# One hybrid decoder step on one core: VectorE's work in the recurrence in program order, some operations handed out later

## The chip, the cores and the metric

One core of a Trainium2 chip runs the whole program. The metric is the device time of one execution in microseconds; three executions of the kernel before gave 1235.94, 1236.01 and 1239.28 us (median 1236.01).

## The reference, cut to what matters

576 tokens (512 of a prompt, 64 of eight sample sequences) go through one layer with three branches, all from one input projection. Everything is fp32.

```
xn = RMSNorm(x);  proj = xn @ w_in                      # 105 column blocks of 128
y_conv = B * conv3(C * h) * silu(g_conv)
y_rwkv = RWKV7(token-shifted r, k, v, decay, icl) * silu(g_rwkv)
y_mem  = softmax(q K^T / sqrt(d)) V * silu(g_mem)       # 4 heads, 256 memory tokens
merged = sum_i sigmoid(m_i) * (y_i @ w_branch[i])
y = RMSNorm_final(x + merged @ w_out)

# RWKV7, for each of 16 heads, one token after another:
sa = S @ kk
S  = S * w  - outer(sa, kk * a) + outer(v, k)
o  = S @ r
```

## The kernel before, in words

**Products.** A product (`mm`, line 233) takes 128 columns of a weight against the 576 tokens. Each fp32 operand is split into a high and a low part, so a product is 48 matmuls of 128 x 288: eight blocks of the contraction, three terms, two halves of the tokens. `mm` yields after each pair of matmuls. One such yield is called a **step** here: a product is 24 steps, two matmuls each.

**Lanes.** `drive` (line 278) runs a main generator; after each of its steps it gives each of five lanes one turn, in the order chain, post, merge, invert, prep. A lane that yields n sits out n turns, so `yield n` puts n + 1 steps between what is before it and after it. So the matmuls of the recurrence come between the matmuls of the products, at places that count in steps, not in time.

**The order on each engine.** Around everything stands `tc.manual_schedule(engines=MANUAL)` with TensorE alone (line 31): TensorE takes its instructions in the order in which the program hands them out. The order on VectorE, ScalarE, GpSimd and the DMA queues is the framework's planner's, which places instructions when it thinks that their inputs are there. Each engine's queue then runs in the order so fixed, each instruction waiting for its own inputs.

**The recurrence** is done in chunks of 64 tokens, nine to a pair of heads (eight of the prompt, one for all samples), for eight pairs of heads p = 0 to 7. `rwkv_main` (line 950) gives it its main stream: first `lora`, then for each p the projections of r, k (after `want[0] >= p`) and v, and between them a filler: eight convolution blocks of four products, eight queries, then tanh gates for the later branches (`early_gates`, list `EARLY`, line 403) for as long as any lane is busy. A gate made early is stored to DRAM and fetched by `branch` (line 1014); one that was not made early is computed there. For a pair p:

- `shift` (line 421) mixes a projected tile with its predecessor token: ScalarE writes `E`, VectorE copies two edges out of PSUM (lines 431, 432) and combines tile and `E` (lines 437 to 445). `proj` marks the tile in `got`.
- `prep` (line 565) makes decays, keys and masks: exponentials on ScalarE, a scan, then `while moved[0] < p - 1 or done[0] < p - 1` (chain p - 2 must be over), four wide operations (lines 613 to 617: `fkb`, `fva`, `eF`, `fkb`), 9 steps later the matmuls of line 633, masks `msk`, and DMAs through DRAM (`scr`) into `nin`. Then it sets `want` and queues `invert`.
- `invert` (line 686): yields 28, then solves 32 x 32 triangles in 31 dependent rounds, `tmp = Z * nin` and `Z = Z - tmp` (lines 696, 698), both on VectorE, one round per step (`yield 0`). DMAs through `sco` put the result into `msk`. It queues `merge` with a due step 92 steps on (`READY`).
- `merge` (line 711): after the due step two VectorE transposes of `msk` (line 786), matmuls (lines 796, 803), and so on; 25 steps after the due step `chain` is queued.
- `chain` (line 833): nine chunks of 16 steps. In each, line 869 multiplies by the state `sb`, VectorE adds the result into `vu` (line 871), 8 steps later lines 882 and 887 use `vu`, VectorE updates `sb` in two operations (line 893), and 8 steps later line 869 of the next chunk uses `sb`. So every 8 steps TensorE needs what VectorE was given 8 steps before. One chain runs at a time.
- `post` (line 907): sample states and the group norm.

After the recurrence come attention beside branch 0, then gates and branches 2 and 1 as plain products, then the output product with `wout`'s weights and the final norm.

Of the kernel before, what the change touches and what calls it, by code (L numbers as in the profile page):

```python
# [61 lines left out]
def pr(t):  # L62
    return v3(t)[:, :, 0:256]
# [22 lines left out]
def hybrid_step(ctx, tc, x_nat, x_t, mem_t, w_in, w_br, w_mk, w_mv, w_o, kc, vc, swkv,  # L86
# [188 lines left out]
    chain_lane, post_lane, prep_lane, inv_lane, mrg_lane = (Lane() for _ in range(5))  # L275
    lanes = [chain_lane, post_lane, mrg_lane, inv_lane, prep_lane]

    def drive(main):
        for _ in main:
            TICK[0] += 1  # L280
            for ln in lanes:
                ln.step()

# [116 lines left out]
    def etile(tag, dt=F32, **k):  # L400
        return el.tile([128, T], dt, name="e" + tag, tag=tag, **k)

    EARLY = [(i, j) for i in (1, 2) for j in range(8)]
    gates = {}
    QT = ("r", "k", "A", "B", "C", "D", "E1", "F")
    qt = []
# [9 lines left out]
    with ExitStack() as rctx:  # L416
# [4 lines left out]
        def shift(ps, idx, out, flat=True):  # L421
            E = shf.tile([128, 513 + 72], F32, name="E", tag="E")
            Es = E[:, 513:585].rearrange("p (b t) -> p b t", t=9)
            mu = pc("mu", idx)
            G.memset(E[:, 0:1], 0.0)
            act(E[:, 1:513].rearrange("p (h t) -> p h t", h=2), ps[:, :, 0:256], scale=mu)
            act(Es[:, :, 0:1], shp[:, idx, :].unsqueeze(2), scale=mu)
            for hf in range(2):
                act(Es[:, 4 * hf:4 * hf + 4, 1:9],
                    ps[:, hf, 256:288].rearrange("p (b t) -> p b t", t=8), scale=mu)  # L430
            V.tensor_copy(sho[:, idx, 0:1], ps[:, 1, 255:256])
            V.tensor_copy(sho[:, idx, 1:9].rearrange("p (h b) -> p h b", h=2),
                          ps[:, :, 256:288].rearrange("p h (b t) -> p h b t", t=8)[:, :, :, 7])
            om = omm[:, idx:idx + 1]
            if flat:
                out = c9(out)
                stt(out[:, 0:8].rearrange("p (h c) t -> p h (c t)", h=2), ps[:, :, 0:256], om,
                    E[:, 0:512].rearrange("p (h t) -> p h t", h=2), ALU.mult, ALU.add)
            for hf in range(2):
                if not flat:  # L440
                    stt(out[:, 4 * hf:4 * hf + 4], c9(ps[:, hf, 0:256]), om,
                        c9(E[:, 256 * hf:256 * hf + 256]), ALU.mult, ALU.add)
                stt(out[:, 8, 32 * hf:32 + 32 * hf].rearrange("p (b t) -> p b t", t=8),
                    ps[:, hf, 256:288].rearrange("p (b t) -> p b t", t=8), om,
                    Es[:, 4 * hf:4 * hf + 4, 0:8], ALU.mult, ALU.add)

        def conv(j):
            U = cvp.tile([128, 514 + 80], F32, name="U")
            Us = U[:, 514:594].rearrange("p (b t) -> p b t", t=10)
            G.memset(U[:, 0:2], 0.0)  # L450
            G.tensor_copy(Us[:, :, 0:2], scv[:, j])
            ps = yield from mm(w_in[WC + j])
            c = cvp.tile([128, T], F32, name="c")
            act(v3(c), m3(ps))
            yield "tile"
            ps = yield from mm(w_in[WH + j])
            tt(V, U[:, 2:514].rearrange("p (h t) -> p h t", h=2), ps[:, :, 0:256], pr(c), ALU.mult)
            for hf in range(2):
                tt(V, Us[:, 4 * hf:4 * hf + 4, 2:10],
                   ps[:, hf, 256:288].rearrange("p (b t) -> p b t", t=8),  # L460
                   v3(c)[:, hf, 256:288].rearrange("p (b t) -> p b t", t=8), ALU.mult)
            G.tensor_copy(cvo[:, j, 0:2], U[:, 512:514])
            G.tensor_copy(cvo[:, j, 2:18].rearrange("p (b t) -> p b t", t=2), Us[:, :, 8:10])
            if j == 6:
                yc.extend(slots("s3b", 2))
            y = yc[j]
            w = [pc("cw%d" % i, j) for i in range(3)]

            def up(i):
                return U[:, i:i + 512].rearrange("p (h t) -> p h t", h=2)  # L470

            def us(i, hf):
                return Us[:, 4 * hf:4 * hf + 4, i:i + 8]

            def ys(hf):
                return v3(y)[:, hf, 256:288].rearrange("p (b t) -> p b t", t=8)

            cb = pc("conv_b", j)
            act(pr(y), up(0), AF.Identity, scale=w[0], bias=cb)
            for hf in range(2):  # L480
                act(ys(hf), us(0, hf), AF.Identity, scale=w[0], bias=cb)
            for i in (1, 2):
                stt(pr(y), up(i), w[i], pr(y), ALU.mult, ALU.add)
                for hf in range(2):
                    stt(ys(hf), us(i, hf), w[i], ys(hf), ALU.mult, ALU.add)
            yield "tile"
            ps = yield from mm(w_in[WB + j])
            stt(v3(y), m3(ps), 0.5, v3(y), ALU.mult, ALU.mult)
            yield "tile"
            ps = yield from mm(w_in[WG + j])  # L490
            th = cvp.tile([128, T], F32, name="c")
            act(v3(th), m3(ps), AF.Tanh, scale=0.5)
            stt(v3(th), v3(th), 1.0, m3(ps), ALU.add, ALU.mult)
            tt(G, y, y, th, ALU.mult)
            yield "tile"


# [17 lines left out]
        def lora():  # L515
            act(blkr, cc("blk"))
            ps = yield from mm(w_in[WP + 24])

            lor, swp = etile("A"), etile("B")
            shift(ps, 24, lor)  # L520
            act(lor[up], lor[up], AF.Tanh)
            S.dma_start(out=swp[dn], in_=lor[up])
            S.dma_start(out=swp[up], in_=lor[dn])
            stacks(lx, lor, swp)
            for o, (a, b) in enumerate(((lor, swp), (swp, lor))):
                tt(V, xlo[o][up], a[up], lx[o][up].bitcast(F32), ALU.subtract)
                tt(V, xlo[o][dn], b[dn], lx[o][dn].bitcast(F32), ALU.subtract)
# [24 lines left out]

        def proj(p, i):
            ps = yield from mm(w_in[WP + 8 * i + p])
            if i < 2:
                t = etile("rk"[i])
                shift(ps, 8 * i + p, t)
            else:
                t = fvas[p]
                shift(ps, 8 * i + p, t[:, :, 0, :], flat=False)  # L560
            got[p, i] = t

        got, fvas = {}, {}

        def prep(p):
            r, k = got[p, 0], got[p, 1]
            fs = slice(p * 128, p * 128 + 128)
            A = etile("A")
# [20 lines left out]
            act(D, D, AF.Exp, scale=CD / 2)  # L589
            act(F, k, scale=pc("k_k", p))  # L590
            act(E1, B, AF.Identity, scale=kah[:, p:p + 1], bias=kah[:, 8 + p:9 + p])
            yield 3
            tt(V, E1, E1, k, ALU.mult)
            act(A, A, AF.Exp, scale=-CD / 2)

# [88 lines left out]
            yield 0  # L684

        def invert(p, msk, mu_, nin, sco, fkb, fva, pcl, rn):
            yield 28

            zp = pch.tile([128, 512], F32, name="c")
            Z = zp[0:108, 0:352].rearrange("p (m k) -> p m k", k=32)  # L690
            tmp = rw.tile([108, 11 * 32], F32, name="tmp", bufs=1)
            act(zp[0:108, 0:352], zini)
            for j in range(31):
                nm, nk = j // 3 + 1, 31 - j
                tv = tmp[:, 0:nm * nk].rearrange("p (m k) -> p m k", k=nk)
                tt(V, tv, Z[:, 0:nm, j:j + 1].to_broadcast([108, nm, nk]),
                   nin[:, j:j + 1, j + 1:32].to_broadcast([108, nm, nk]), ALU.mult)
                tt(V, Z[:, 0:nm, j + 1:32], Z[:, 0:nm, j + 1:32], tv, ALU.subtract)
                yield 0
            sq3 = sco.rearrange("u (m q) k -> q u m k", q=3)  # L700
            act(tmp, zp[0:108, 0:352])
            zo = tmp.rearrange("p (m k) -> p m k", k=32)
            for q in range(3):
                S.dma_start(out=sq3[q], in_=zo[36 * q:36 * q + 36])
            for bl in range(2):
                q0 = 64 + 32 * bl
                S.dma_start(out=mu_[q0:q0 + 32, :, 32 * bl:32 * bl + 32],
                              in_=sco[18 * bl:18 * bl + 18, 0:32, :].rearrange("u s t -> s u t"))
            mrg_lane.q.append(merge(p, msk, fkb, fva, pcl, rn, TICK[0] + READY))
# [197 lines left out]
        def post(p, S0, vu8, chk8, pcl):  # L907
# [19 lines left out]
            V.tensor_reduce(st[:, 0, :], of, axis=AX.X, op=ALU.add)  # L927
            V.tensor_scalar(st[:, 0, :], st[:, 0, :], 1.0 / 64, None, op0=ALU.mult)
            tt(G, of, of, st[:, 0, :].unsqueeze(2).to_broadcast([128, 10, 64]), ALU.subtract)
            yield 1  # L930
            sq = rw.tile([128, 10, 64], F32, name="sq", tag="mb", bufs=1)
            act(sq, of, AF.Square)
            V.tensor_reduce(st[:, 1, :], sq, axis=AX.X, op=ALU.add)
            G.tensor_scalar(st[:, 1, :], st[:, 1, :], 1.0 / 64, 64e-5, op0=ALU.mult, op1=ALU.add)
            tt(G, st[:, 2, :], st[:, 1, :], nhalf[:, 0:10], ALU.pow)
# [58 lines left out]
                else:  # L994
                    return

        drive(rwkv_main())

    S.dma_start(out=o_conv, in_=cvo)
    S.dma_start(out=o_shift, in_=sho)  # L1000
# [256 lines left out]
            yield lag  # L1257


    prep_lane.q.append(wout(0, 27))  # L1260
    drive(branch(1, *parts, merged=(mgh, mgl)))
    for _ in wout(1, 0):
        pass
# [139 lines left out]
```

## Time and profile before

| | before |
|---|---|
| median of three executions | 1236.01 us |
| profiled execution, its own time | 1235.45 us |
| its span, first to last instruction | 1233.6 us |
| TensorE busy | 1186.9 us, 96% of the span |
| VectorE, ScalarE, GpSimd busy | 587.0, 524.9, 573.8 us |
| mean granted TensorE clock | 0.994 |

The profiled execution's own time is 1.85 us over its span (what lies ahead of the first and behind the last instruction). Matmuls overlap in TensorE's pipeline and their ends are modelled, so idle time of TensorE is a wait, while a busy TensorE is not one at its peak. Lines 93, 96 and 99 are helpers (`tt`, `stt`, `act`) that issue most of the work of VectorE, GpSimd and ScalarE; there the tiles' names tell which operation it is. In them `e` stands ahead of tiles of `etile`, and `c`, `tmp`, `nin` are the inversion's `Z`, `tmp`, `nin`.

### The profile page before, as it was taken

How to read it: one execution, taken by the hardware profiler on the slowest of the kernel's cores; microseconds unless marked ns; L12 is line 12 of the kernel's file. 1: busy time of each engine (PE TensorE's matmuls, PEld its weight loads, DVE VectorE, ACT ScalarE, POOL GpSimd, SP SyncE). 2: the span in 40 equal slices, each digit the busy share in tenths (PEclk: the TensorE clock that was granted, in tenths of full speed). 3: DMA queues.
4: the chain of work that ended last, by engine and by line, in shares of the span. 5: the costliest groups of instructions: out<-in, count | busy, mean ns of one | idle time of the engine just before them, and what ended most of it. 6: DMA issues, size and time to landing. Idle time of an engine off the chain costs nothing. (4 is left out here: it accounts for less than half of the span.)

```text
span 1233.6 us, 25594 instructions
## 1 busy us (share of the span) xinstructions
PE 1186.9 (96%) x10158; PEld 1100.8 (89%) x10158; DVE 587.0 (48%) x1514; ACT 524.9 (43%) x1120; POOL 573.8 (47%) x521
## 2 busy tenths in 40 slices
PE   7999979999899999999989999999999999999997
PEld 7798979989798988988879898889899999999976
DVE  7856866468675686647673315213113100134233
ACT  6563446435463544546344435333233222233222
POOL 4535532555535465454543545333334454446642
PEclk9999989999999999999999999999999999999999
DMA  8642222132321322222322225653632222225522
GB/s 290 213 126 72 70 72 63 59 91 58 91 65 53 89 68 84 90 86 70 110 80 74 69 71 171 195 181 123 208 97 87 80 84 86 78 86 161 161 105 78
DMA packets 93056, 129.39 MB, mean 105 GB/s; under 512 B 36988, under 2 KB 41320, under 8 KB 92936
## 3 DMA queue, kind: packets, MB, share of 16 engines
q1 hardware_dynamic: 55888, 110.20, 28.3%
q10 hardware_dynamic: 37048, 17.56, 5.4%
q8 instruction: 80, 1.31, 0.5%
q14 instruction: 40, 0.33, 0.1%
HBM read 115.96 MB, written 11.47 MB: 103 GB/s over the span
## 5 line engine op out<-in xcount | busy, mean ns | idle before, releaser
L93 POOL TENSOR_TENSOR wl<-w,wh 128x512 fp32r<-128x512 f32 x274 | 366.5, 1340 | 490.0 <-ACT wh L99 451.4
L245 PE MATMUL m<-xh,wh 128*128 128x288 f32 x1680 | 370.4, 302 | 0.5 <-ACT vst L99 0.5
L245 PE MATMUL m<-xl,wh 128*128 128x288 f32 x1680 | 369.4, 301 | 0.0
L245 PE MATMUL m<-xh,wl 128*128 128x288 f32 x1680 | 365.2, 299 | 0.0
L99 ACT ACTIVATE wh<-w 128x512 fp32r<-128x512 f32 x290 | 180.5, 627 | 294.2 <-PE m L245 169.1
L245 PEld LDWEIGHTS m<-xh,wh 128*128 128x128 f32 x1680 | 268.8, 189 | 8.6 <-issue 3.7
L245 PEld LDWEIGHTS m<-xl,wh 128*128 128x128 f32 x1680 | 269.2, 189 | 6.4 <-issue 2.9
L245 PEld LDWEIGHTS m<-xh,wl 128*128 128x128 f32 x1680 | 269.4, 189 | 3.0 <-issue 2.1
L96 DVE SCALAR_TENSOR_TENSOR ev<-ev,m 128x576 f32<-128x576 f32 x32 | 24.2, 755 | 168.4 <-PE m L245 110.3
L245 PE MATMUL m<-yh,wh 128*128 128x288 f32 x384 | 82.9, 297 | 0.0
L245 PE MATMUL m<-yh,wl 128*128 128x288 f32 x384 | 82.8, 297 | 0.0
L245 PE MATMUL m<-yl,wh 128*128 128x288 f32 x384 | 82.8, 297 | 0.0
L245 PEld LDWEIGHTS m<-yh,wl 128*128 128x128 f32 x384 | 61.7, 188 | 2.1 <-issue 2.1
L245 PEld LDWEIGHTS m<-yl,wh 128*128 128x128 f32 x384 | 61.7, 188 | 2.1 <-issue 2.1
L245 PEld LDWEIGHTS m<-yh,wh 128*128 128x128 f32 x384 | 61.7, 189 | 2.1 <-issue 2.1
L93 DVE TENSOR_TENSOR c<-c,tmp 108x84 f32<-108x84 f32 (+23 forms) x248 | 56.6, 228 | 5.4
L93 DVE TENSOR_TENSOR tmp<-c,nin 108x84 f32<-108x84 f32 (+23 forms) x248 | 54.8, 221 | 6.7 <-issue 1.2
L96 DVE SCALAR_TENSOR_TENSOR sb<-o,pcl,sb 64x64 f32<-64x64 f32 x112 | 31.6, 282 | 52.1 <-PE o L887 46.0
L99 ACT ACTIVATE osb<-o 64x128 f32<-64x128 f32 x72 | 19.7, 274 | 52.3 <-DVE sb L96 30.5
L93 DVE TENSOR_TENSOR vu<-o,vu 64x128 f32<-64x128 f32 x56 | 15.9, 284 | 46.6 <-PE o L869 45.6
L99 ACT ACTIVATE E<-m,par 128x32 f32<-128x32 f32 (+1 forms) x75 | 27.2, 418 | 22.2 <-PE m L245 14.1
L99 ACT ACTIVATE sb<-sb,pcl 128x128 f32<-128x128 f32 x56 | 22.5, 401 | 29.4 <-DVE sb L96 18.8
(441 smaller groups left out, 1796.2 us busy)
## 6 DMA issues: line engine op xcount, KB each, us to landing
w<-w_in_in SPq DMA_DIRECT2D x210, 256.0 KB
w<-w_br_in SPq DMA_DIRECT2D x48, 256.0 KB
kb<-kc_in SPq DMA_DIRECT2D x16, 512.0 KB
kb<-vc_in SPq DMA_DIRECT2D x16, 512.0 KB
w<-w_mk_in SPq DMA_DIRECT2D x16, 256.0 KB
w<-w_mv_in SPq DMA_DIRECT2D x16, 256.0 KB
w<-w_o_in SPq DMA_DIRECT2D x16, 256.0 KB
nin<-scr ACTq DMA_DIRECT2D x24, 144.0 KB
```

The costliest lines, as they stand in the source:

```text
L93: e.tensor_tensor(out=out, in0=a, in1=b, op=op)
L96: V.scalar_tensor_tensor(out=out, in0=a, scalar=s, in1=b, op0=op0, op1=op1)
L99: S.activation(out, in_, f, **k)
L245: TE.matmul(ps[:, hf, :n], a[:, f], b[:, k, hf * n:hf * n + n], start=(k == 0 and i == 0), stop=(k == 7 and i == 2))
```

## The change

The recurrence is put into `tc.manual_schedule` for VectorE too: in it VectorE takes its instructions in the order in which the program hands them out. Some operations that take results of ScalarE or GpSimd are handed out some steps later, through a list `later` that `drive` empties by step, or by longer yields: the mixing of `shift` and the mark in `got` by 5 steps, the convolution's taps by 5, its gate's silu by 4; `prep` yields 9 in place of 3 ahead of line 593; `invert` yields 34 in place of 28; `post` yields 6 in place of 1 and 4 more. The list of early gates begins with branch 2, and the step between the loads of `wout` is worked out from the number of gates left.

```diff
+    later = []
+    def defer(n, fn):
+        later.append((TICK[0] + n, fn))
+        later.sort(key=lambda x: x[0])
     def drive(main):
         for _ in main:
             TICK[0] += 1
+            while later and later[0][0] <= TICK[0]:
+                later.pop(0)[1]()
             for ln in lanes:
                 ln.step()
...
-    EARLY = [(i, j) for i in (1, 2) for j in range(8)]
+    EARLY = [(i, j) for i in (2, 1) for j in range(8)]
...
         def shift(ps, idx, out, flat=True):
...
+            def mix():            # the three or four scalar_tensor_tensor of before
...
+            return mix
...
         def conv(j):
...
+            def taps():           # the six scalar_tensor_tensor of before
...
+            defer(5, taps)
...
+            def silu():
+                stt(v3(th), v3(th), 1.0, m3(ps), ALU.add, ALU.mult)
+                tt(G, y, y, th, ALU.mult)
+            defer(4, silu)
...
         def proj(p, i):
             ps = yield from mm(w_in[WP + 8 * i + p])
+            t = etile("rk"[i]) if i < 2 else fvas[p]
+            mix = shift(ps, 8 * i + p, t if i < 2 else t[:, :, 0, :], flat=i < 2)
+            def finish():
+                mix()
+                got[p, i] = t
+            defer(5, finish)
...
         def prep(p):
+            while (p, 0) not in got or (p, 1) not in got:
+                yield 0
...
             act(E1, B, AF.Identity, scale=kah[:, p:p + 1], bias=kah[:, 8 + p:9 + p])
-            yield 3
+            yield 9
             tt(V, E1, E1, k, ALU.mult)
...
         def invert(p, msk, mu_, nin, sco, fkb, fva, pcl, rn):
-            yield 28
+            yield 34
...
             tt(G, of, of, st[:, 0, :].unsqueeze(2).to_broadcast([128, 10, 64]), ALU.subtract)
-            yield 1
+            yield 6
             sq = rw.tile([128, 10, 64], F32, name="sq", tag="mb", bufs=1)
             act(sq, of, AF.Square)
+            yield 4
             V.tensor_reduce(st[:, 1, :], sq, axis=AX.X, op=ALU.add)
...
-        drive(rwkv_main())
+        with tc.manual_schedule(engines={mybir.EngineType.DVE}):
+            drive(rwkv_main())
+            assert not later
...
-    prep_lane.q.append(wout(0, 27))
+    nt = 16 - sum((1, j) in gates for j in range(8))
+    prep_lane.q.append(wout(0, min(27, (24 * nt - 16) // 8 - 1)))
```

## Rows read from the trace of the kernel before

**Rows 1.** The page, busy time of each engine.
```profile
PE 1186.9 (96%) x10158; PEld 1100.8 (89%) x10158; DVE 587.0 (48%) x1514; ACT 524.9 (43%) x1120; POOL 573.8 (47%) x521
```
**Rows 2.** Windows: length, busy us by engine, clock; the recurrence, the late products.
```profile
74.00:748.00 674.00, 645.60 (x6287) 597.45 (x6287) 409.21 (x1228) 322.14 (x739) 331.49 (x325) 0.99 0.27 78
...
907.00:1172.00 265.00, 265.00 (x1990) 265.00 (x1989) 59.27 (x75) 82.75 (x144) 133.10 (x100) 1.00 0.33 101
```
**Rows 3.** Waits of TensorE in the recurrence, us in total, times, longest.
```profile
PE s L796 <- DVE ts L93: 5.5, 1, 5.5
PE s L633 <- DVE fkb L96: 2.6, 2, 1.4
PE o L869 <- DVE sb L96: 2.3, 3, 1.2
```
**Rows 4.** Waits of VectorE in the recurrence.
```profile
DVE sb L96 <- PE o L887: 46.0, 31, 3.5
...
DVE t L786 <- DMA msk<-sco: 13.2, 6, 7.7
```
**Rows 5.** Timeline of VectorE, 150 to 185 us: start, length, operation, idle before.
```profile
159.12 0.18 DVE L93 TENSOR_TENSOR c<-c,tmp 108x11 f32<-108x11 f32 x1
167.00 0.76 DVE L786 STREAM_TRANSPOSE t<-msk 32x256 f32<-32x256 f32 x2 [7.71 <-DMA msk<-sco]
```
**Rows 6.** Windows of 5 us around that wait; the clock is third last.
```profile
165.00:170.00 5.00, 0.28 (x20) 0.28 (x24) 2.95 (x12) 2.19 (x6) 2.53 (x3) 0.73 0.37 81
170.00:175.00 5.00, 5.00 (x79) 4.59 (x72) 3.78 (x21) 2.74 (x8) 1.28 (x1) 0.59 0.33 106
```
**Rows 7.** A window of 20 us with shorter waits, same columns.
```profile
560.00:580.00 20.00, 17.77 (x138) 16.69 (x138) 15.51 (x66) 10.98 (x25) 6.88 (x8) 1.00 0.20 66
```
**Rows 8.** DMA issues of the early gates.
```profile
L504 ACTq DMA_DIRECT2D gate<-c x7: 326/344/453, 515.3 to 604.1; - x7
```
**Rows 9.** Groups of VectorE by line and tile: count, busy us, mean ns, idle before.
```profile
L93 DVE TENSOR_TENSOR c<-c,tmp 108x84 f32<-108x84 f32 (+23 forms) x248 | 56.6, 228 | 5.4
L93 DVE TENSOR_TENSOR tmp<-c,nin 108x84 f32<-108x84 f32 (+23 forms) x248 | 54.8, 221 | 6.7 <-issue 1.2
L96 DVE SCALAR_TENSOR_TENSOR sb<-o,pcl,sb 64x64 f32<-64x64 f32 x112 | 31.6, 282 | 52.1 <-PE o L887 46.0 <-ACT E L99 2.1 <-ACT gn L99 1.9
...
L93 DVE TENSOR_TENSOR vu<-o,vu 64x128 f32<-64x128 f32 x56 | 15.9, 284 | 46.6 <-PE o L869 45.6
...
L96 DVE SCALAR_TENSOR_TENSOR fkb<-eB,eF 128x576 f32<-128x576 f32 x8 | 11.9, 1488 | 0.1
...
L93 DVE TENSOR_TENSOR fva<-eF,eA 128x576 f32<-128x576 f32 x8 | 10.6, 1322 | 0.2
...
L93 DVE TENSOR_TENSOR eF<-eF,eD 128x576 f32<-128x576 f32 x8 | 9.2, 1150 | 0.1
L96 DVE SCALAR_TENSOR_TENSOR er<-m,omm,E 128x32 f32<-128x32 f32 (+1 forms) x24 | 9.0, 409 | 0.0
...
L93 DVE TENSOR_TENSOR fkb<-eE,eD 128x576 f32<-128x576 f32 x8 | 8.9, 1110 | 0.1
```
**Rows 10.** Timeline of VectorE, rounds of an inversion that follow one another.
```profile
643.13 0.23 DVE L93 TENSOR_TENSOR tmp<-c,nin 108x72 f32<-108x72 f32 x1
643.40 0.24 DVE L93 TENSOR_TENSOR c<-c,tmp 108x72 f32<-108x72 f32 x1
643.68 0.22 DVE L93 TENSOR_TENSOR tmp<-c,nin 108x64 f32<-108x64 f32 x1
643.93 0.23 DVE L93 TENSOR_TENSOR c<-c,tmp 108x64 f32<-108x64 f32 x1
644.20 0.22 DVE L93 TENSOR_TENSOR tmp<-c,nin 108x63 f32<-108x63 f32 x1
```
**Rows 11.** Timeline of TensorE, half a chunk of a chain.
```profile
644.45 0.38 PE L887 MATMUL o<-vu,chk 128*128 128x128 f32 x2
...
646.78 0.38 PE L869 MATMUL o<-sb,fva 128*128 128x128 f32 x2
```

More of the change, by code (lines that the diff above doesn't have):

```diff
@@ L434, in shift @@
             om = omm[:, idx:idx + 1]
[L435 to L445, printed above, removed]
+            def mix():
+                o = c9(out) if flat else out
+                if flat:
+                    stt(o[:, 0:8].rearrange("p (h c) t -> p h (c t)", h=2), ps[:, :, 0:256], om,
+                        E[:, 0:512].rearrange("p (h t) -> p h t", h=2), ALU.mult, ALU.add)
+                for hf in range(2):
+                    if not flat:
+                        stt(o[:, 4 * hf:4 * hf + 4], c9(ps[:, hf, 0:256]), om,
+                            c9(E[:, 256 * hf:256 * hf + 256]), ALU.mult, ALU.add)
+                    stt(o[:, 8, 32 * hf:32 + 32 * hf].rearrange("p (b t) -> p b t", t=8),
+                        ps[:, hf, 256:288].rearrange("p (b t) -> p b t", t=8), om,
+                        Es[:, 4 * hf:4 * hf + 4, 0:8], ALU.mult, ALU.add)
+            return mix
         def conv(j):
@@ L481, in conv @@
                 act(ys(hf), us(0, hf), AF.Identity, scale=w[0], bias=cb)
[L482 to L485, printed above, removed]
+            def taps():
+                for i in (1, 2):
+                    stt(pr(y), up(i), w[i], pr(y), ALU.mult, ALU.add)
+                    for hf in range(2):
+                        stt(ys(hf), us(i, hf), w[i], ys(hf), ALU.mult, ALU.add)
+            defer(5, taps)
             yield "tile"
@@ L492, in conv @@
             act(v3(th), m3(ps), AF.Tanh, scale=0.5)
-            stt(v3(th), v3(th), 1.0, m3(ps), ALU.add, ALU.mult)
-            tt(G, y, y, th, ALU.mult)
+            def silu():
+                stt(v3(th), v3(th), 1.0, m3(ps), ALU.add, ALU.mult)
+                tt(G, y, y, th, ALU.mult)
+            defer(4, silu)
             yield "tile"
@@ L519, in lora @@
             lor, swp = etile("A"), etile("B")
-            shift(ps, 24, lor)
+            shift(ps, 24, lor)()
             act(lor[up], lor[up], AF.Tanh)
@@ L554, in proj @@
             ps = yield from mm(w_in[WP + 8 * i + p])
[L555 to L561, printed above, removed]
+            t = etile("rk"[i]) if i < 2 else fvas[p]
[4 more added lines that the diff above has]
+            defer(5, finish)
         got, fvas = {}, {}
         def prep(p):
+            while (p, 0) not in got or (p, 1) not in got:
+                yield 0
             r, k = got[p, 0], got[p, 1]
```

## The prediction

> **What bounds the kernel now.** I read the page's busy times first: TensorE is busy 96% of the span, the other three under half [rows 1]. So time is gained only where TensorE waits, and lost where it is made to wait. The table by stage shows where it waits: in the recurrence, 74 to 748 us, it is idle 674.0 - 645.6 = 28.4 us; in the late products, 907 to 1172 us, it is idle nowhere [rows 2]. The change touches the recurrence's order, so 28.4 us of waits, and what they cost in clock, is all that there is to gain.
>
> The waits of TensorE by releaser show one of 5.5 us at line 796 and small ones behind `fkb` and `sb` [rows 3]. What is behind the long one is seen on VectorE: it ends the first inversion at 159.3 us, takes the transposes of line 786 next and stands 7.71 us until the DMA from `sco` has landed [rows 5]. Line 796 stands 92 steps behind the inversion in the program; the planner had let the inversion fall back until the slack was gone. Over all pairs line 786 waits 13.2 us [rows 4]. During the long wait the clock falls: 0.73 and then 0.59 in the two stretches of 5 us around its end [rows 6], mixtures of TensorE's two levels, 2.4 and 1.2 GHz.
>
> On the other side VectorE waits 46.0 us for line 887 before `sb` [rows 4] and as long for line 869 before `vu` [rows 9]: in the chain it is usually early.
>
> **The change, part by part.**
>
> *Length in steps.* Seven gates were made early [rows 8], so the stretch held 1 + 24 + 32 + 8 + 7 = 72 products, 1,728 steps, in 674 us [rows 2]: 0.39 us a step with everything between. From the yields: the first chain starts at step 304. Chain q starts 200 steps after chain q - 2 ends (prep's tail 23, invert 29 + 31, due step 92, merge 25) and runs 152, so chains q and q - 2 lie 352 apart; chain 1 follows chain 0 at 456, chain 7 starts at 456 + 3 x 352 = 1512 and ends at 1664, `post` at 1713; the next end of a product is 1728, as counted. With the change the first chain is 18 steps later (invert 6, prep 6, `got` with its turn 6), the cycle is 6 longer three times, `post` 10 longer: 1713 + 18 + 18 + 10 = 1759, rounded to 1776, 74 products. So nine gates are made early, the eight of branch 2 and one of branch 1. Products move from the late stages into the recurrence; none is added, and TensorE has them back to back there [rows 2]. Two more gates mean two stores and two loads; DMA is 27% busy in the recurrence and 33% late [rows 2]. With 15 gates of branch 1 and products left, the `wout` step stays 27. All this I cost at nothing; without that cover it would be a product's wait on a gate, of which no row shows any.
>
> *The late inversion.* In program order an inversion ends near its own steps, and line 786 comes 92 steps, some 36 us, later. The DMA takes 7.7 us of that [rows 5]. The wait of 5.5 us goes. In the 5 us after it, at 0.59 and with TensorE busy throughout, 0.41 x 5 = 2.0 us of work are lost. So 7.5 us are saved here. Of the other 28.4 - 5.5 = 22.9 us of waits, those that follow the late inversions and the planner's misjudged order go, those at an operation that simply takes long stay. Bounds 0 and 22.9; with no row that splits them I take half, 11. Gain 18.5 us (7.5 to 30.4).
>
> *The inversion in a burst.* An inversion is 31 rounds in 31 steps of the program. In the kernel before VectorE spreads it over whatever time is free. In program order it can't: whatever is handed out at a later step stands behind the round of that step. One round takes 228 + 221 ns [rows 9], and with the gap before each instruction (643.13 to 644.20 us are two rounds) 0.53 us at that size [rows 10]; I take 0.449 + 2 x 0.03 = 0.51, 15.8 us for 31. In the same 31 steps lie two chunks of a chain, two `vu` at 284 ns and four `sb` at 282 ns [rows 9], 1.7 us, and 31/24 of a projection's mixing, three operations at 409 ns, 1.6 us. Together VectorE is given 19.1 us of work.
>
> TensorE would pass these 31 steps much faster. Eight steps of a chain with nothing else took 2.33 us, line 887 at 644.45 to line 869 at 646.78 [rows 11], 0.29 a step, 9.0 us for 31; at the mean of 0.39 it would be 12.1. It can't run away from VectorE, since line 869 needs the `sb` that was handed out 8 steps before, and line 887 the `vu`. That gives a slack of 8 steps less the operation itself (0.6): 1.7 us, or 2.5 at the mean step. So per burst TensorE stands 19.1 - 9.0 - 1.7 = 8.4 us at the fast step, 19.1 - 12.1 - 2.5 = 4.5 at the mean one; I take 6.5, between the two, since the mean step holds today's waits and work outside the bursts as well. A chain runs during the burst of p = 2 to 7: the burst lies 36 to 67 steps after `want` is set, which is steps 59 to 90 of the chain of p - 1 for even p and some 5 to 36 for odd p. Six bursts: 39 us. At p = 1 chain 0 hasn't started, but merge 0 (lines 786 to 809) runs with slacks of 5 to 8 steps; I take 3. At p = 0 only products run, whose PSUM tiles VectorE must free within 19 steps, and I take nothing. Sum 42 us (0 if TensorE's slack proves enough; 7 x 8.4 = 59 above).
>
> *The wide operations.* The four of lines 613 to 617 take 1.11 + 1.32 + 1.15 + 1.49 = 5.1 us [rows 9] and line 633 follows 9 steps, 2.6 to 3.5 us, later. The planner could put them ahead, since their inputs are early; program order puts them behind the last `vu` of the chain before, 8 steps earlier still. 17 steps cover them, 9 don't: 0 to 2.5 us for each of 8 pairs. Nearest to the 2.6 us in two waits of now [rows 3], I take 0.5 more each: 4 us.
>
> *The deferrals.* `shift`'s mix, taps and silu come 4 to 6 steps later, and the next product that needs their PSUM tile comes 24 steps after it, so 18 steps, 7 us, are left; nothing. `invert`'s extra 6 are for `nin`: if its DMA were still late, the first round would stand, and behind it on VectorE `vu` and `sb`, for which TensorE waits. The rounds wait 6.7 us in all now [rows 9]; I leave this at nothing, and a microsecond late would be up to one for a pair.
>
> *Sum.* 1235.45 (the profiled execution, 0.6 under the median) - 18.5 + 42 + 4 = 1263 us.
>
> **The rivals.**
>
> *Faster: the bursts are hidden.* If VectorE did a round in the time in which TensorE passes a step, nothing but the saved waits would be left: 1235.45 - 18.5 = 1217 us, with 1205 and 1228 at the gain's bounds. It decides at 0.51 us a step. For it: the mean step is 0.39, not 0.29, a burst that starts with VectorE ahead has more slack, and VectorE waits 46 us for line 887 today [rows 4]. Against: 0.39 is still under 0.51 before anything else is counted.
>
> *The clock falls in the bursts.* Of the 5 us after the long wait TensorE ran 4.1 at the lower level (half speed there makes the mean 0.59) [rows 6]; in 20 us with 2.2 us of shorter waits the clock stayed at 1.00 [rows 7]. A burst's waits are 2 to 3 us each, three in a row, between the two cases. If each of seven bursts ended as that wait did, at 2 us, it would be 14 us more, 1277 us. The Trainium skill (TensorE: Matmul & The Clock Gate, section HAM oscillation) says that waits which come back again and again let the clock fall and climb anew each time, and that this price is then paid each time. By that rule this is the likelier of the two slow cases; the trace has one such fall in the recurrence of the length needed, and the shorter waits speak against it.
>
> *It does little.* The planner's order may be near program order already, and gain and burst may cancel: 1236 us.
>
> **How the numbers follow.** Bursts without a fall of the clock 0.50, with it 0.12, hidden bursts 0.28, no change 0.10. The likeliest is 1263. Its own range is 1243 to 1286: the sum with bursts at 4.5 and at 8.4 us is 1251 and 1274 (wide operations and p = 1 as above), and the gain's half-width of 11 us is let in by 8 to 12 at either end. The range must take in most of the faster case too, so 1214 to 1286; below lies about a third of that case, above some of the one with the clock. What can be told from no change here is about 0.3%, 1232.3 to 1239.7. Slower: 0.62; same 0.10; faster 0.28.
>
> **What would show it.** Right: no wait at line 796 behind line 786; each inversion over in 16 to 22 us; in these stretches VectorE above 90% busy and TensorE idle 5 to 9 us, waiting at lines 869, 882 and 887 for `sb` and `vu`; nine gate stores; idle time of TensorE in the recurrence about 60 us. Wrong, if TensorE isn't idle there: then the slack of the chain was misread, or a round is shorter than 0.51 us when VectorE works in order. It would also be wrong if VectorE stood at `nin` or behind ScalarE at its new places, which would cost more than is counted here.

## The result and the profile after

The changed kernel took 1303.45 us (median of four, 1302.33 to 1304.99) against 1235.97 us of the kernel before (median of four): ratio 1.0554, 95% interval 1.0536 to 1.0572. It is 67 us slower. Slower was forecast, but by 28 us, and 1303 lies outside the range.

The page of the kernel after, its first part; before it was [rows 1]:

```profile
span 1300.5 us, 25598 instructions
...
PE 1210.3 (93%) x10158; PEld 1119.7 (86%) x10158; DVE 607.4 (47%) x1514; ACT 526.4 (40%) x1120; POOL 572.1 (44%) x521
```

The number of matmuls is the same, 10,158, so the time is not more work but waits and a lower clock. The recurrence with its two more products now lasts to about 844 us (windows: length, busy us and instructions of PE, PEld, DVE, ACT, POOL, then the clock, DMA share and GB/s):

```profile
74.00:844.00 770.00, 699.02 (x6498) 646.71 (x6497) 440.63 (x1244) 336.37 (x763) 345.62 (x335) 0.96 0.25 74
```

TensorE is idle 770.0 - 699.0 = 71.0 us in it, where it was 28.4 [rows 2]: 42.6 us more. The mean granted clock over the span fell from 0.994 to 0.974, which is (1 - 0.974) x 1300.5 = 33.8 us of full clock missing against (1 - 0.994) x 1233.6 = 7.4: 26.4 us more. The two make 69.0; the span grew by 66.9, since some of the slow clock fell into waits.

Where TensorE waits in the recurrence after (us in total, times, longest), against [rows 3]; lines 889, 902, 907, 653 and 816 are now what 869, 882, 887, 633 and 796 were:

```profile
PE s L653 <- DVE fkb L96: 16.4, 6, 4.8
PE o L889 <- ACT osb L99: 10.1, 6, 2.2
PE o L889 <- DVE sb L96: 8.6, 4, 2.5
PE s L697 <- POOL eA L93: 4.8, 5, 1.2
PE o L902 <- DVE vu L93: 4.5, 2, 3.4
...
PE s L816 <- DVE t L806: 0.7, 1, 0.7
```

The long wait of before, 5.5 us at line 796, is 0.7 us at most. In its place stand the wide operations (`fkb`) and the chain's own round trip (`sb`, `vu`). The name `osb` at line 889 is the last release by the profile, ScalarE's copy of the product of the chunk before. In the burst shown below that copy had itself waited for VectorE's `sb`.

**A burst.** The inversions of p = 2, 4 and 6, start of the first round to the end of the slack behind the last one:

```profile
290.90:312.40 21.50, 15.70 (x120) 14.89 (x119) 19.28 (x78) 10.61 (x24) 5.36 (x6) 1.00 0.15 52
...
459.90:481.40 21.50, 17.13 (x112) 16.38 (x111) 19.28 (x78) 10.74 (x24) 5.30 (x6) 0.86 0.15 51
...
630.70:652.10 21.40, 17.05 (x120) 16.31 (x119) 19.18 (x78) 10.72 (x24) 5.31 (x6) 0.92 0.16 50
```

VectorE is 90% busy and TensorE idle 4.4 to 5.8 us in each; the rounds of p = 2 themselves took 18.7 us. Over all eight such stretches TensorE was idle 32.0 of 181.1 us: 0.1 us at p = 0, 4.9 at p = 1, and 3.5 to 5.8, 4.5 in the mean, at p = 2 to 7. Inside one, the timeline of VectorE in the kernel after, from the middle of the burst of p = 2:

```profile
293.74 0.28 DVE L93 TENSOR_TENSOR vu<-o,vu 64x128 f32<-64x128 f32 x1
294.06 0.24 DVE L93 TENSOR_TENSOR tmp<-c,nin 108x75 f32<-108x75 f32 x1
...
298.26 0.26 DVE L93 TENSOR_TENSOR c<-c,tmp 108x90 f32<-108x90 f32 x1
298.43 0.57 DVE L96 SCALAR_TENSOR_TENSOR sb<-o,pcl,sb 64x64 f32<-64x64 f32 x2
```

and of TensorE:

```profile
296.27 0.42 PE L245 MATMUL m<-xh,wh 128*128 128x288 f32 x2
299.15 0.46 PE L889 MATMUL o<-sb,fva 128*128 128x128 f32 x2 [2.46 <-DVE sb L96]
```

Between `vu` and the next `sb` VectorE does eight rounds, 294.06 to 298.43 us, 0.55 us each. TensorE came to line 889 at 296.7, stood 2.46 us and started within 0.2 us of the end of `sb`. This is the mechanism of the forecast, and a wait of the length that it gave to one (2 to 3 us); a whole burst was forecast at 6.5 us and has 4.5. The last wait of this burst has the name `osb`. VectorE's `sb`, ScalarE's copy and TensorE, in this order:

```profile
308.58 0.57 DVE L96 SCALAR_TENSOR_TENSOR sb<-o,pcl,sb 64x64 f32<-64x64 f32 x2
309.19 0.56 ACT L99 ACTIVATE osb<-o 64x128 f32<-64x128 f32 x2 [1.02 <-DVE sb L96]
309.80 0.49 PE L889 MATMUL o<-sb,fva 128*128 128x128 f32 x2 [2.20 <-ACT osb L99]
```

**The wide operations and the clock.** VectorE at p = 1 in the kernel after, then TensorE, then windows of 5 us:

```profile
149.00 1.33 DVE L93 TENSOR_TENSOR eE<-eE,ek 128x576 f32<-128x576 f32 x1
150.34 0.35 DVE L624 TENSOR_SCALAR rn<-s 64x10 f32<-64x10 f32 x2
...
150.99 0.76 DVE L93 TENSOR_TENSOR fkb<-eE,eD 128x576 f32<-128x576 f32 x1
151.67 1.83 DVE L93 TENSOR_TENSOR fva<-eF,eA 128x576 f32<-128x576 f32 x1
153.53 0.76 DVE L93 TENSOR_TENSOR eF<-eF,eD 128x576 f32<-128x576 f32 x1
154.33 0.76 DVE L96 SCALAR_TENSOR_TENSOR fkb<-eB,eF 128x576 f32<-128x576 f32 x1
```

```profile
155.23 1.19 PE L653 MATMUL s<-fva,fkb 64*128 64x128 f32 x7 [4.77 <-DVE fkb L96]
```

```profile
150.00:155.00 5.00, 0.46 (x4) 0.22 (x2) 4.86 (x8) 1.52 (x3) 1.77 (x3) 0.62 0.33 82
155.00:160.00 5.00, 4.77 (x27) 4.58 (x28) 2.12 (x4) 0.00 (x0) 1.40 (x1) 0.50 0.00 0
```

VectorE never pauses here; it is behind, with the burst of p = 0 just over, and TensorE waits 4.77 us for the last wide operation. Then the clock is at 0.50, its lower level of 1.2 GHz, for 5 us, of which TensorE works 4.77. One wait of 4.8 us cost 0.5 x 4.77 = 2.4 us more by the clock in this window alone.

What VectorE does ahead of the wide operations differs from pair to pair. At p = 1 it is mostly earlier work of the same `prep`. At p = 2 and p = 4 (VectorE):

```profile
256.29 3.59 DVE L96 SCALAR_TENSOR_TENSOR ts3c<-U,par,ts3c 128x512 f32<-128x512 f32 x6 [0.41 <-POOL cvo L475]
259.80 0.75 DVE L93 TENSOR_TENSOR fkb<-eE,eD 128x576 f32<-128x576 f32 x1
...
426.00 0.69 DVE L93 TENSOR_TENSOR chk<-s,rn 64x512 f32<-64x512 f32 x1 [3.34 <-ACT chk L99]
426.70 0.76 DVE L93 TENSOR_TENSOR fkb<-eE,eD 128x576 f32<-128x576 f32 x1
```

At p = 2 these are 3.6 us of the convolution's taps, which the change hands out later. At p = 4 VectorE stands 3.34 us for ScalarE in front of `chk`, and the wide operations stand behind it in the queue; p = 6 is the same (3.35 us).

### The profile page after: what moved, and what is told of

Read it like the earlier page. It is cut to its first block, busy times and chain, and to the rows that moved or that the text cites. A ratio compares the mean times of both kernels' runs of the same rounds, so it can differ in the third digit from the quotient of the medians.

```text
span 1300.5 us, 25598 instructions
## 1 busy us (share of the span) xinstructions
PE 1210.3 (93%) x10158; PEld 1119.7 (86%) x10158; DVE 607.4 (47%) x1514; ACT 526.4 (40%) x1120; POOL 572.1 (44%) x521
## 4 chain that ended last, share of the span: by engine, by line
PE 66%; DVE 11%; issue 4%; POOL 3%; ACT 2%; ACTq 1%; DMA 0%; POOLq 0%; DVEq 0%
PE m L245 49%; PE m L1308 4%; DVE tmp L93 3%; DVE c L93 3%; PE s L1113 2%; PE o L902 1%; PE o L907 1%; PE s L653 1%; POOL wl L93 1%; PE o L889 1%; PE c L1183 1%; PE o L1216 1%; PE s L863 1%; PE s L775 1%; DVE msk L93 1%
## 5 line engine op out<-in xcount | busy, mean ns | idle before, releaser
L245 PE MATMUL m<-xl,wh 128*128 128x288 f32 x1680 | 376.6, 306 | 0.0
L245 PE MATMUL m<-xh,wl 128*128 128x288 f32 x1680 | 374.7, 305 | 0.6 <-POOL wl L93 0.6
L245 PEld LDWEIGHTS m<-xl,wh 128*128 128x128 f32 x1680 | 274.2, 193 | 8.8 <-issue 6.8
L245 PEld LDWEIGHTS m<-xh,wh 128*128 128x128 f32 x1680 | 275.1, 193 | 7.2 <-issue 2.1
L245 PEld LDWEIGHTS m<-xh,wl 128*128 128x128 f32 x1680 | 274.8, 193 | 6.2 <-issue 2.1
L96 DVE SCALAR_TENSOR_TENSOR ev<-ev,m 128x576 f32<-128x576 f32 x32 | 24.1, 754 | 152.9 <-PE m L245 94.4
L889 PE MATMUL o<-sb,fva 128*128 128x128 f32 x112 | 22.8, 285 | 18.8 <-ACT osb L99 10.1
L93 DVE TENSOR_TENSOR msk<-s,con 128x512 f32<-128x512 f32 (+1 forms) x48 | 24.6, 551 | 29.3 <-PE s L653 24.5
```

Source lines behind the costliest of these rows:

```text
L93: e.tensor_tensor(out=out, in0=a, in1=b, op=op)
L96: V.scalar_tensor_tensor(out=out, in0=a, scalar=s, in1=b, op0=op0, op1=op1)
L245: TE.matmul(ps[:, hf, :n], a[:, f], b[:, k, hf * n:hf * n + n], start=(k == 0 and i == 0), stop=(k == 7 and i == 2))
L889: TE.matmul(po[:, cols], wr.rearrange("p n t -> p (n t)"), cur, start=(c == g0), stop=False, skip_group_check=True)
```

## The experiments

Twelve kernels, each timed beside the kernel before. Ratios are to the kernel before in the same runs; "program order" and "planner's order" are VectorE's in the recurrence.

### Order and steps apart

The change with the planner's order kept:

```diff
-        with tc.manual_schedule(engines={mybir.EngineType.DVE}):
-            drive(rwkv_main())
-            assert not later
+        drive(rwkv_main())
+        assert not later
```

> The changed kernel with VectorE's order given back to the planner; all deferrals, longer yields and the order of the gates stay. Theory A (the loss is VectorE's program order): back to the kernel before, 1225 to 1245 us, TensorE idle under 35 us in the recurrence. Rival B (the loss is in the later steps and longer yields): stays over 1280 us.

Measured: 1219.29 us, ratio 0.9860 (0.9845 to 0.9874). Rival B falls. A holds for the cause, but 1219 lies under its 1225 to 1245: this is not the kernel before again but a faster one than it. Its recurrence, nine early gates included (windows):

```profile
74.00:760.00 686.00, 669.64 (x6504) 623.41 (x6503) 426.41 (x1244) 338.92 (x767) 351.15 (x335) 1.00 0.28 84
```

16.4 us idle, and the clock back at 0.994 over the span.

The other corner, the kernel before with VectorE in program order and nothing else:

```diff
-        drive(rwkv_main())
+        with tc.manual_schedule(engines={mybir.EngineType.DVE}):
+            drive(rwkv_main())
```

> The kernel before, with VectorE in program order in the recurrence and nothing else of the change: no deferral, the old yields. The changed kernel with the planner's order took 1219 us, so program order costs 84 us at the new steps. Theory A (order costs, and the later steps help under either order): 1236 + 84 = 1320 us or somewhat more, since in program order an operation that waits for ScalarE holds the whole queue. Rival B (the later steps help under the planner alone and are a loss in program order): under 1300 us.

Measured: 1343.54 us, ratio 1.0875 (1.0859 to 1.0892). This is theory A, 24 us above its 1320. Its recurrence, 800 us, and the waits of TensorE at line 796 in it:

```profile
74.00:874.00 800.00, 703.16 (x6417) 648.14 (x6416) 425.27 (x1243) 334.59 (x760) 338.15 (x331) 0.94 0.24 69
```

```profile
PE s L796 <- DVE msk L93: 8.4, 3, 2.8
...
PE s L796 <- DVE ts L93: 2.5, 1, 2.5
```

With the order alone VectorE no longer waits for the DMA from `sco` (13.2 us before), but line 796 still waits, 10.9 us in all, now for VectorE's own work.

| us, median | planner's order | program order | order costs |
|---|---|---|---|
| steps of before | 1236.0 | 1343.5 | 107.5 |
| later steps | 1219.3 | 1303.5 | 84.2 |
| later steps gain | 16.7 | 40.0 | |

So the change is two changes of opposite sign. The order alone costs over 100 us; the later steps take some of it back, and would be a gain with the order left alone.

### The bursts: half as dense, twice as dense

One round every second step, the due step moved so that nothing after it shifts:

```diff
                 tt(V, Z[:, 0:nm, j + 1:32], Z[:, 0:nm, j + 1:32], tv, ALU.subtract)
-                yield 0
+                yield 1
...
-        READY = 92
+        READY = 61
```

> The changed kernel, but the inversion does one round every second step (62 steps in place of 31) and merge's due step comes 61 in place of 92 steps after it, so that every later step stays where it was. Theory A, part 1 (31 rounds in 31 steps give VectorE more than TensorE's chain leaves time for; 32 us of idle TensorE in the eight bursts, and clock): 25 us of those waits go and about half of the 23 us that the lower clock costs, about 1265 us. Rival B: within 5 us of 1303.

Measured: 1269.53 us, ratio 1.0265 (1.0250 to 1.0280), 34 us under the changed kernel. The same three pairs' inversions, p = 2, 4 and 6:

```profile
285.40:310.50 25.10, 23.46 (x192) 22.14 (x191) 22.77 (x85) 14.15 (x31) 10.71 (x10) 1.00 0.19 64
444.80:468.60 23.80, 22.82 (x188) 21.50 (x187) 21.47 (x84) 13.44 (x30) 9.34 (x9) 1.00 0.21 68
606.00:629.80 23.80, 22.82 (x188) 21.51 (x187) 21.48 (x84) 13.43 (x30) 9.34 (x9) 1.00 0.26 80
```

VectorE is as busy as in the changed kernel, 90%, but TensorE is idle only 1.0 to 1.6 us in each and passes 190 matmuls in place of 112 to 120. At p = 3, 5 and 7 the gain is small (3.2 to 3.8 us idle for 3.5 to 5.0 in the changed kernel); over all eight stretches, which now hold twice the steps, it is 19.5 of 227.5 us. Over the recurrence its idle time is 51.2 us, 20 less, and the mean clock over the span is 0.985, 15 us less missing: together about the 34.

Two rounds in a step:

```diff
-                yield 0
+                if j % 2:
+                    yield 0
...
-        READY = 92
+        READY = 108
```

> The changed kernel with two rounds of the inversion in each step, 15 steps in place of 31, and merge's due step 108 in place of 92 steps after it. Theory A (a burst costs VectorE's work less the time in which TensorE passes the steps): TensorE's time for 16 steps, some 4.6 to 6 us, is no longer set against the burst, so 3 to 5 us more in each of six or seven bursts, 1320 to 1335 us, clock included. Rival B (the bursts are not what costs): within 5 us of 1303.

Measured: 1330.66 us, ratio 1.0773 (1.0755 to 1.0790), 27 us over the changed kernel, as theory A had it. Two of its bursts, p = 2 and 4:

```profile
296.70:316.00 19.30, 12.35 (x63) 11.51 (x62) 17.04 (x73) 5.41 (x13) 3.99 (x4) 0.73 0.14 43
476.20:495.00 18.80, 10.98 (x60) 10.25 (x59) 16.54 (x71) 5.39 (x13) 3.99 (x4) 0.77 0.13 43
```

TensorE is idle 7.0 and 7.8 us in them, nearly all of it in two waits each, at the lines that are 907 and 889 in the changed kernel. TensorE at p = 2; at p = 4 the two are 3.16 and 4.67 us:

```profile
303.22 0.80 PE L908 MATMUL o<-vu,chk 128*128 128x128 f32 x2 [3.16 <-DVE vu L93]
312.50 0.80 PE L890 MATMUL o<-sb,fva 128*128 128x128 f32 x2 [3.79 <-DVE sb L96]
```

The clock inside these two bursts is 0.73 and 0.77, where it was 1.00 and 0.86 in the changed kernel. Half, one and two rounds a step give 1270, 1303 and 1331 us: the density of the bursts is shown to be a cause.

### The wide operations

```diff
             G.tensor_copy(pcl[:, 8:16], C[:, 512:576].rearrange("p (c t) -> p c t", t=8)[:, :, 7])
-            yield 8
+            yield 18
```

> The changed kernel, but 18 in place of 8 is yielded between the four wide VectorE operations of prep and the matmuls that read them. Theory A, part 2 (in program order the wide operations start only behind the last vu of the chain before): the 16.4 us of waits at those matmuls go, and about 8 us of clock with them, about 1280 us; the bursts stay. Rival B: within 5 us of 1303, the wait only appears elsewhere.

Measured: 1296.97 us, ratio 1.0484 (1.0466 to 1.0502), only 6.5 us under the changed kernel. The waits of TensorE in its recurrence:

```profile
PE o L889 <- ACT osb L99: 13.4, 7, 2.8
PE o L902 <- DVE vu L93: 8.3, 6, 2.8
PE o L889 <- DVE sb L96: 5.4, 3, 2.1
PE o L907 <- DVE vu L93: 5.3, 3, 2.8
...
PE s L653 <- ACT chs L99: 3.8, 3, 2.5
```

The 16.4 us at the wide operations are gone as expected, but idle time fell by 5.8 us only, to 778.00 - 712.76 = 65.2 us:

```profile
74.00:852.00 778.00, 712.76 (x6605) 659.07 (x6605) 434.45 (x1236) 343.32 (x773) 348.29 (x340) 0.96 0.25 74
```

The result lies closer to rival B than to theory A. Other waits grew: those for `osb`, `vu` and `sb` at lines 889, 902 and 907 are 32.4 us here and 26.6 in the changed kernel, and the eight stretches of the bursts have 36.3 us of idle time in place of 32.0. These waits do not stand directly behind the wide operations: in the 15 us after each of the eight sets of them TensorE has no wait of 0.9 us or more at these lines. So it is not shown that the wide operations hold up the chain's `vu` and `sb`. The edit also lengthens the cycle by ten steps a pair (eleven early gates in place of nine) and so moves the chain against the bursts; which of its effects brought the new waits was not tried. With both edits:

> Both edits, every second step and 18 after the wide operations. Theory A: the two gains add up, about 1240 us, TensorE idle some 30 us in the recurrence and its clock there at 0.99 as in the kernel before. If the clock falls for another reason than these waits (rival C), the waits go and the clock stays at 0.96, about 1262 us.

Measured: 1271.55 us, ratio 1.0282 (1.0266 to 1.0297), no better than the spread alone. Neither theory had that; the two gains don't add up. The waits at the wide operations fall from 14.2 to 0.7 us, and yet idle time in the recurrence is 48.6 us against 51.2 of the spread alone: almost as much came back elsewhere, at lines 889, 907, 816 and at 653 itself, there for ScalarE's `chs` (3.8 us). Handing the readers out later moved the wait and hardly reduced it.

### Copies left at the head of the queue

`shift`'s two edge copies weren't deferred by the change, and in program order VectorE stands 28.8 us in them for ScalarE. Deferred with the mixing:

```diff
-            V.tensor_copy(sho[:, idx, 0:1], ps[:, 1, 255:256])
-            V.tensor_copy(sho[:, idx, 1:9]...
...
             def mix():
+                V.tensor_copy(sho[:, idx, 0:1], ps[:, 1, 255:256])
+                V.tensor_copy(sho[:, idx, 1:9]...
```

> The changed kernel, with the two edge copies of shift deferred along with its mixing. In program order they were left where they stood, and VectorE waits 28.8 us in them for ScalarE's E. Theory A, part 3 (whatever waits at the head of VectorE's queue holds the chain's vu and sb behind it): 8 to 15 us less, 1288 to 1295 us. Rival: these waits are VectorE's spare time and hide nothing that TensorE needs, 1301 to 1305 us.

Measured: 1295.82 us, ratio 1.0495 (1.0480 to 1.0511), 7.6 us less. Its recurrence:

```profile
74.00:838.00 764.00, 691.65 (x6506) 639.57 (x6505) 441.99 (x1244) 339.54 (x767) 344.54 (x335) 0.97 0.25 75
```

TensorE is idle 72.3 us in it, and was 71.0 in the changed kernel: the gain is in the clock (699.0 us of busy time became 691.7), not in waits. On top of the spread:

> The changed kernel with one round every second step (1270 us) and the edge copies deferred. Theory A, part 3: 8 to 15 us less than 1270. Rival: 1268 to 1272 us. Neither theory expects the 1219 us of the planner's order, since the wide operations still start late (14 us of waits).

Measured: 1264.08 us, ratio 1.0230 (1.0208 to 1.0252), 5.5 us less. Here idle time did fall, from 51.2 to 45.8 us. Both gains are clear of the noise, so the rival falls, and both lie under the 8 us at the lower end of theory A. That the copies hold up `vu` and `sb`, as theory A says, the first of the two traces does not show. This is the best that was found in program order, 45 us over the planner's order with the same steps.

### What the planner gains from later steps

The longer yields without the deferrals, and the deferrals without the longer yields, both in the planner's order and with the new order of the gates; and that order of the gates alone:

```diff
-            yield 28
+            yield 34
...
-            yield 3
+            yield 9
...
-            yield 1
+            yield 6
...
+            yield 4
```

> The kernel before (planner's order) with the longer yields in invert, prep and post and the new order of the gates, without the deferrals. Theory A (what the planner gains is the inversion handed out 6 steps later, so that it isn't started ahead of its data and merge's transposes don't hold VectorE): most of the 17 us, 1219 to 1225 us. Rival D (the deferrals gain it): 1233 to 1238 us.

> The changed kernel with the planner's order and the old yields: the deferrals alone (and the new order of the gates). Theory A (yields): 1232 to 1238 us. Rival D (deferrals): 1219 to 1225 us.

> The kernel before with nothing but the new order of the early gates (and the loads of wout spaced by the gates left). Every theory: no product is added or taken away and TensorE has them back to back late, so 1234 to 1238 us. Were it 1230 us or less, part of the gains of the yields alone (1229) and of the deferrals alone (1225) would belong to the gates.

Measured: yields alone 1228.63 us, ratio 0.9943 (0.9928 to 0.9958); deferrals alone 1224.76, 0.9912 (0.9895 to 0.9928); the gates alone 1235.09, 1.0001 (0.9991 to 1.0010). The yields gain 7 us, between the ranges of the two theories, and the deferrals 11, as rival D had it; together about the 17. The new order of the gates costs and brings nothing, as forecast. (Seven gates are made early in that run, so the two more of the change are not tried by it.)

```diff
-            defer(5, finish)
+            defer(9, finish)
...
-            defer(5, taps)
+            defer(9, taps)
...
-            defer(4, silu)
+            defer(8, silu)
```

> The changed kernel with the planner's order (1219 us) and the deferrals longer: mixing and taps by 9 in place of 5 steps, silu by 8 in place of 4. If the planner gains from the deferrals because it misjudges when ScalarE's results come, a longer one helps once more, 1212 to 1217 us. If 5 and 4 steps were enough, 1218 to 1222 us.

Measured: 1230.10 us, ratio 0.9962 (0.9947 to 0.9977): neither. Still later is 11 us worse than 5 and 4 steps, with TensorE idle 21.1 us from 74 to 760 us in place of 16.4 and the clock at 0.987 in place of 0.994; why stays open. The best version of the study is the change without its order, 1219.29 us.

## Why the prediction was wrong in size and right in sign

- *Length in steps.* Right: nine gates were made early, and their new order alone costs no time (1.0001).
- *The late inversion.* Its 5.5 us went, as forecast, and so did VectorE's waits for the DMA from `sco`. The reason given, program order, is half of it: with the order alone line 796 still waits 10.9 us, while in the planner's order with the later steps VectorE still waits 6.8 us for that DMA and TensorE not at all at this line. The further 11 us that I took for "the planner's misjudged order" did not come: with program order alone idle time rose by 68 us, to 96.8. Something was there to gain, 17 us, but the planner's order gets it by the later steps, which I had costed at nothing.
- *The bursts.* Right in place and mechanism (density halved and doubled: 34 us less, 27 us more), and the idle time was less than I had: 32.0 us in eight stretches for a forecast of 42. The six with a chain in them have 4.5 us in the mean, the lower of the two figures between which I took 6.5. What was missing is the clock; spreading the rounds gave back 20 us of idle time and 15 of clock.
- *The wide operations.* Mis-sized: 4 us forecast on top of 2.6, 16.4 seen. I gave them 17 steps of cover, as if VectorE were free when the last `vu` of the chain before is done. In program order it isn't: earlier work stands ahead of them (149.00 to 150.99 us at p = 1, the taps at p = 2) or an operation that waits for ScalarE (p = 4 and 6). The deferrals I had costed at nothing, and VectorE standing behind ScalarE I had named as a sign of being wrong and given no price.
- *The step that failed: "it would be 14 us more".* I kept the fall of the clock as a rival at 0.12 beside the sum, in seven bursts at 2 us each. It is part of the likeliest case: 26.4 us. The price of a fall was about right and the count was wrong. In windows of 5 us from 74 us to the end of the recurrence the clock is under 0.9 in 14 separate places, in the kernel before in two. By the table below the twelve more cost 33.8 - 5.9 = 27.9 us without the first 74 us, about 2.3 us each. Seven of the 14 lie in a burst's stretch or at most 10 us behind it; four stand at a wait for the wide operations, which the rival did not count. Nor does a fall need a wait of 5.5 us: after the wait of 2.22 us for the wide operations at p = 3 the clock is 0.89 and 0.76. A wait of that size doesn't always bring one: after 2.79 us at 602.85 the clock stayed at 1.00. Over the kernels the missing clock follows idle time, loosely (missing is (1 - clock) x span; the first 74 us lie ahead of the recurrence and differ from profile to profile):

| | idle TensorE in the recurrence | mean clock over the span | clock missing, us | of it in the first 74 us |
|---|---|---|---|---|
| later steps, planner's order | 16.4 | 0.994 | 7.3 | 5.2 |
| before | 28.4 | 0.994 | 7.4 | 1.5 |
| change, spread and copies | 45.8 | 0.981 | 24.0 | 5.2 |
| change, spread and wide | 48.6 | 0.981 | 24.1 | 5.2 |
| change, spread | 51.2 | 0.985 | 19.0 | 3.7 |
| change, wide | 65.2 | 0.972 | 36.3 | 6.7 |
| change | 71.0 | 0.974 | 33.8 | 0.0 |
| change, copies | 72.3 | 0.978 | 28.5 | 6.7 |
| change, two rounds a step | 89.4 | 0.957 | 57.2 | 5.2 |
| order alone | 96.8 | 0.960 | 53.7 | 5.2 |

By the rule of the Trainium skill (TensorE: Matmul & The Clock Gate, section HAM oscillation), weighed above, recurring waits pay for the clock each time. These runs agree in the main. Without the first 74 us, between 28 and 97 us of idle time each further microsecond of waiting came with about 0.6 of missing clock (48.5 - 5.9 = 42.6 us of clock over 96.8 - 28.4 = 68.4 of waits). Single kernels lie up to 11 us off that line, the copies alone furthest below it: the sum of the waits does not decide it alone.

- *Taken together.* Forecast: idle +29.5 (-16.5 + 42 + 4) and clock -2. Measured: idle +42.6 and clock +26.4. Sizing the clock by this ratio, which only the runs give, 0.6 x 29.5, would have made the sum 1235.45 + 29.5 + 17.7 = 1283 us; most of the rest is the wide operations and the gain that didn't come.
- *Faster, and no change* fell with the result: the slack of 8 steps does not cover eight rounds.

Open: program order with the rounds spread and the copies deferred is still 45 us over the planner's order with the same steps. Its trace has 733.0 - 687.2 = 45.8 us of idle time in the recurrence, 13.9 of them at the wide operations, and 24 us of clock missing, against 16.4 and 7.3. That adds up (29.4 + 16.7), but which places in VectorE's queue would have to move was not tried further.

## What to carry to other kernels

An order written out in program steps is as good as the step counts are in time: before fixing an engine's order, compare for each stretch the work handed to it per step with the time in which the engine that sets the pace passes a step, and look at what is queued behind the densest piece and behind each operation that may wait for another engine. When a change makes TensorE wait often, add to the waits the clock that they cost, in the likeliest case and not as a remote one. And take a change of order and the delays that come with it apart: here the delays were worth 17 us in the planner's order, and program order cost 84.

## What the runs showed of the hardware that was not expected

The clock was lost to shorter waits than the one of 5.5 us in the kernel before. Behind one of 4.77 us it stood at 0.50 for 5 us in which TensorE worked almost throughout, and in bursts with TensorE idle 7 to 8 of 19 us, in waits of 3.2 to 4.7 us, it was 0.73 to 0.77, while stretches with 1.0 to 1.6 us idle in 24 or 25 kept 1.00. The burst of p = 2 in the changed kernel, 5.8 us idle in 21.5 in pieces of up to 2.5, still ran at 1.00. Behind it the clock fell twice (windows, changed kernel):

```profile
315.00:320.00 5.00, 3.81 (x36) 3.47 (x35) 4.12 (x8) 2.02 (x4) 4.18 (x3) 0.85 0.19 30
320.00:325.00 5.00, 5.00 (x52) 4.45 (x51) 0.57 (x2) 1.86 (x5) 0.36 (x2) 0.81 0.14 52
325.00:330.00 5.00, 5.00 (x52) 4.88 (x48) 0.28 (x1) 1.75 (x4) 4.34 (x5) 1.00 0.41 107
...
335.00:340.00 5.00, 2.78 (x25) 2.42 (x25) 4.96 (x10) 0.43 (x1) 1.52 (x3) 0.89 0.28 87
340.00:345.00 5.00, 4.85 (x33) 3.59 (x31) 1.88 (x3) 0.00 (x0) 0.00 (x0) 0.76 0.00 0
```

```profile
316.38 0.46 PE L889 MATMUL o<-sb,fva 128*128 128x128 f32 x2 [1.19 <-DVE sb L96]
337.47 1.16 PE L653 MATMUL s<-fva,fkb 64*128 64x128 f32 x16 [2.22 <-DVE fkb L96]
```

The first fall came after a wait of only 1.19 us at 316.38, 6.6 us behind the end of the one of 2.20 at 309.80; the second, with full speed between them, after the wait for the wide operations of p = 3.
